# Key norm weights applied behind the transposition, and one finishing of the branch gates, in a hybrid attention layer

## The chip, the core and the metric

The kernel runs on one core of one Trainium2 chip. A core has five engines that run their own instruction streams and wait for each other by semaphores: TensorE (PE, matrix products and transpositions), VectorE (DVE), ScalarE (ACT), GpSimd (POOL) and SyncE (SP, which here issues transfers). The metric is the device time of one execution in microseconds (us). Some executions are also recorded by the hardware profiler; the span in a profile runs from the first to the last instruction.

## The reference

One decoder layer with 512 tokens, width 1024, heads of 64, all in float32. Two mixers read the same normalized input through one projection; their outputs are gated, projected and merged. Cut to what the change touches:

```python
def rms_norm(x, g):
    return x * lax.rsqrt(jnp.mean(x * x, axis=-1, keepdims=True) + EPS) * g

h = rms_norm(x, norm_w)
(q_a, k_a, v_a, z_a, q_b, kc, vc, ksl, vsl, kwn, vwn, gate_b, z_b, gate_m) = split(h @ w_in)
# mixer A: 8 heads, blocks of 256 keys
o_a = moba_mixer(rms_norm(heads(q_a), q_norm_a), rms_norm(heads(k_a), k_norm_a), heads(v_a), bias_a)
# mixer B: 8 query heads in 2 groups; compressed, selected and windowed keys
k_cmp = rms_norm(compress(heads(kc), ...), k_norm_cmp)
o_b = nsa_mixer(rms_norm(heads(q_b), q_norm_b), k_cmp, v_cmp,
                rms_norm(heads(ksl), k_norm_sel), heads(vsl),
                rms_norm(heads(kwn), k_norm_win), heads(vwn), gate_b, bias_b)
# inside nsa_mixer
g = jax.nn.sigmoid(branch_gate)      # 512 tokens x 8 heads x 3 branches
o = g[..., 0:1] * o_cmp + g[..., 1:2] * o_sel + g[..., 2:3] * o_win
```

The weights `g` of a norm are 64 numbers, one for each place within a head, the same for all tokens and heads. A score is the product of a query and a key, so a weight of the query's norm may as well be multiplied into the key's; the kernel does so.

## The kernel before

Tokens are handled in four tiles of 128. Every float32 product on PE is made of three faster ones: both operands are split into a rounded part and a rest (`wh` and `wl` for weights, `hh` and `hl` for the activations, `ks` and `kx` for keys, `ph` and `pl` for probabilities), and line 386 issues high by high, low by high and high by low. A weight tile arrives in `wr`, is rounded into `wh` by ACT (line 352), or by DVE or POOL (lines 354, 356), and its rest `wl` comes from DVE (line 361). The same goes for `vh` and `vl`, weights of the key compression.

The program is written as streams (projections, attention heads, compression of mixer B's keys) that a planner interleaves while the program is built: every step carries a cost for each engine on which it may run, and the planner puts each step on an engine and at a place in that engine's order by the times that these costs give. On the chip an engine works off its list in that order, so an instruction that waits holds all that is behind it on its engine.

The pieces around the change, by line:

- `load_consts` (line 1547) loads small tables: the tile `cst` (constants with one row for each partition, in two transfers of line 255) and `gn` (six vectors of norm weights, the same in all partitions). Four products on DVE (line 1560) then fold the query's weights and the score's factor 0.125 into the key's weights.
- `proj_norm` (line 737) projects one group of channels and norms it, token tile by token tile: `qk0` and `qk1` (each four query heads and four key heads of mixer A), then `kb` (four keys of mixer B, and its 24 gates a token), then `qb`. `norm` (line 709) is: scaled copy out of PSUM (`nraw`, line 718, ACT), square (720, ACT), sum by heads (721, DVE), factor and addition (426, DVE), inverse root (427, POOL), product with it (723, DVE or POOL), and then, for keys, the product with the weights `gn` (line 726 for mixer A, 729 for `kb`; DVE or POOL, whichever the planner found sooner).
- For `kb`, ACT takes the exponential of the negated gate into a small tile `ge` (line 745), and behind the norm DVE adds 1 (749) and takes the reciprocal (750) into the tile `gate`, 24 columns for each token tile: four such pairs in all.
- `k_pair` (line 969) brings two key heads into the form for scores: four transpositions on PE (`turn`, line 947) into a PSUM bank `pq`, of which 64 partitions belong to each head; two rounded copies for each head on ACT, into both halves of `ks` (line 978); the rest `kx` by a subtraction on DVE (line 980) out of the same bank; a copy of it into `kx`'s other half (line 983, ACT). It is called four times for mixer A and twice for mixer B: 24 copies and 12 subtractions. `k_pair`'s bank is of the kind that `q_pair`, the transpositions `pt` of probabilities and the sums `pu` of the compression (line 873) also use; it is free for the next once the last subtraction has read it.
- Scores: `sps` (lines 1024 and 1025) takes `ks` and `kx` against the split query; DVE adds the bias (`sb`, line 1043), ACT takes the exponential (`P`, line 1058), and PE transposes the probabilities (line 1071).
- Mixer B's small matrices are split too: `xs` (lines 706, 707) from the gathered input of the compression, `hs` (868), `gt` (878 to 882).

Of the kernel before, what the change touches and what calls it, by code (L numbers as in the profile page):

```python
# [19 lines left out]
D = 1024  # L20
# [10 lines left out]
COFF, NCST = {}, 0  # L31
for _n, _w in (("ident", P), ("ii", DH), ("cmask", NT * C32), ("rowv", NT), ("hmask", 2), ("pos", 32), ("w2", 256)):
    COFF[_n] = (NCST, _w)
    NCST += _w
# [72 lines left out]
def hybrid_kernel(ctx: ExitStack, tc: tile.TileContext, x, x0, xT, wtok, wchan, wz, wgate, gains, w1,  # L107
# [307 lines left out]

    ident = cview("ident")
    ii = cview("ii")
    cmask = cview("cmask").rearrange("p (b c) -> p b c", b=NT)
# [290 lines left out]
    def norm(ch, dst, ps, t, H, gi):  # L709
# [14 lines left out]
        if gi == 1:  # L724
            z = out[:, 4:]
            ch.do(either(256), lambda e: e.tensor_mul(z, z, gn[:, 1, :].unsqueeze(1).to_broadcast([P, 4, DH])))
        elif gi:
            z = out.rearrange("p (a b) d -> p a b d", a=2)
            ch.do(either(256), lambda e: e.tensor_mul(z, z, gn[:, gi:gi + 2, :].unsqueeze(2).to_broadcast([P, 2, 2, DH])))

# [6 lines left out]
    def proj_norm(name, gi, tags="gggg"):  # L737
        toks[name] = [None] * NT

        def emit(t, ps):  # L740
            toks[name][t] = att(name, F32)
            ch = Chain(now[0] + 230)
            if name == "kb":
                e_ = sp.tile([P, 24], F32, name=nm("ge"), tag="ge", bufs=4)
                ch.do({"A": 164}, lambda e: e.activation(e_, ps[:, 256:280], AF.Exp, scale=nrx[:, t:t + 1]))
            norm(ch, toks[name][t], ps, t, 4 if name == "kb" else 8, gi)
            if name == "kb":
                def g1(e):
                    e.tensor_scalar_add(e_, e_, 1.0)
                    e.reciprocal(gate[:, :, t], e_)  # L750
                ch.do({"D": 300}, g1)
            ch.mark(f"{name}.{t}")
        yield from gemm_tok(name, emit, tags)
# [214 lines left out]

    def k_pair(boxes, name, col, firsts=None):

# [5 lines left out]
        for r, (ks, kx) in enumerate(kk):  # L976
            for i in range(2):
                c.do({"A": 478}, lambda e, r=r, z=ks[64 * i:64 * i + 64, :]: e.copy(z, pt[64 * r:64 * r + 64, :]))
        for r, (ks, kx) in enumerate(kk):
            c.do({"D": 602}, lambda e, r=r, ks=ks, kx=kx: e.tensor_sub(  # L980
                kx[0:64, :], pt[64 * r:64 * r + 64, :], ks[0:64, :].bitcast(F32)), pt if r else None)
        for r, (ks, kx) in enumerate(kk):
# [176 lines left out]
    def moba_units():  # L1159
        us, qs, ks = [], [], [[], []]  # L1160
        for h in range(8):
            box = {}

            def pre(h=h, box=box):
                yield toks_of(f"qk{h // 4}")
                yield toks_of(f"v{h // 4}")
                if h % 2 == 0:
                    yield from q_pair(qs, f"qk{h // 4}", h % 4 * DH)
                    yield from k_pair(ks, f"qk{h // 4}", 256 + h % 4 * DH)
                yield need("rtab")  # L1170
# [10 lines left out]
    def nsa_units(g):  # L1181
# [3 lines left out]
        def pre0():  # L1185
            yield toks_of("kb")
            if not g:
                both.extend(att("kf").rearrange("p (i b c) -> p i b c", i=2, b=2) for _ in range(2))
                for br in range(2):
                    yield from k_pair(kbox, "kb", P * br, [z[:, :, br, :] for z in both])  # L1190
            yield toks_of("qb")
# [355 lines left out]
    def load_consts():  # L1547
# [11 lines left out]
        for i, k in ((0, 1), (2, 3), (2, 4), (2, 5)):  # L1559
            c.do({"D": 102}, lambda e, i=i, k=k: e.scalar_tensor_tensor(gn[:, k, :], gn[:, i, :], 0.125, gn[:, k, :], op0=ALU.mult,  # L1560
                                                                        op1=ALU.mult))

# [221 lines left out]
def _layout(inp):  # L1784
# [21 lines left out]
    onehot, cd = _consts()  # L1806
    cd.update(pos=posT.reshape(P, -1), w2=w2.reshape(P, -1))
    d = dict(x=f["x"][0], xT=f["x"][0].T[P:],
# [25 lines left out]
```

## Time and profile before

| what | value |
| --- | --- |
| time, median of 3 runs | 452.53 us (452.14 to 452.53) |
| profiled execution, its own time | 451.59 us |
| span in that profile | 449.8 us |
| granted TensorE clock, mean | 1.000 |
| PE busy / DVE / ACT / POOL | 441.8 / 384.0 / 302.9 / 198.9 us |
| products with k's weights (lines 726 and 729) | 9 on DVE, 3 on POOL |
| gate pairs (lines 749 and 750) | 4 on DVE |
| plain copies `ks` (line 978) | 24 on ACT |
| subtractions `kx` (line 980) | 12 on DVE |

Rows of the profile name an instruction as line, engine, operation, written tile `<-` read tiles, with partitions x elements. "Idle before" is the time that the engine stood still just before, with the row that released it. The profiled execution and the runs are separate executions, so a sum made from the profile's durations is held against 451.59, not against the median.

### The profile page before, as it was taken

How to read it: one execution, taken by the hardware profiler on the slowest of the kernel's cores; microseconds unless marked ns; L12 is line 12 of the kernel's file. 1: busy time of each engine (PE TensorE's matmuls, PEld its weight loads, DVE VectorE, ACT ScalarE, POOL GpSimd, SP SyncE). 2: the span in 40 equal slices, each digit the busy share in tenths (PEclk: the TensorE clock that was granted, in tenths of full speed). 3: DMA queues.
4: the chain of work that ended last, by engine and by line, in shares of the span. 5: the costliest groups of instructions: out<-in, count | busy, mean ns of one | idle time of the engine just before them, and what ended most of it. 6: DMA issues, size and time to landing. Idle time of an engine off the chain costs nothing.

```text
span 449.8 us, 8544 instructions
## 1 busy us (share of the span) xinstructions
PE 441.8 (98%) x2779; PEld 394.0 (88%) x2779; DVE 384.0 (85%) x943; ACT 302.9 (67%) x711; POOL 198.9 (44%) x235
## 2 busy tenths in 40 slices
PE   8999999999999999999999999999999999999997
PEld 7878888899778899888999998989988999998886
DVE  5999899899998797788899899977967699899783
ACT  6866778867978798376878677687764355454450
POOL 1153337865675573177675654764850222211000
PEclk9999999999999999999999999999999999999999
DMA  8975746887975879858978876986767878789872
GB/s 262 305 253 187 242 150 213 196 228 187 267 181 165 214 220 270 290 142 202 287 213 204 228 181 170 253 218 156 213 166 174 256 220 253 223 245 290 278 237 95
DMA packets 55086, 98.21 MB, mean 218 GB/s; under 512 B 5313, under 2 KB 9537, under 8 KB 55041
## 3 DMA queue, kind: packets, MB, share of 16 engines
q1 hardware_dynamic: 39808, 68.30, 47.2%
q0 software_dynamic: 7616, 14.68, 20.4%
q10 hardware_dynamic: 7616, 14.68, 9.7%
q8 instruction: 22, 0.36, 0.3%
q14 instruction: 24, 0.19, 0.1%
HBM read 90.69 MB, written 36.31 MB: 282 GB/s over the span
## 4 chain that ended last, share of the span: by engine, by line
PE 77%; DVE 12%; ACT 4%; issue 3%; DMA 2%; POOL 0%; SPq 0%; DVEq 0%; ACTq 0%
PE pgw L386 18%; PE pgt L386 14%; PE pbr L386 9%; PE po L386 9%; PE pgc L386 7%; PE O L1105 6%; PE pt L1071 5%; PE sps L1024 3%; PE sps L1025 3%; DVE wl L361 2%; DMA wr<-in_wgate 2%; DVE sb L1043 1%; DVE pl L1085 1%; DVE sq L490 1%; PE pq L947 1%
## 5 line engine op out<-in xcount | busy, mean ns | idle before, releaser
L361 DVE TENSOR_TENSOR wl<-wr,wh 128x512 fp32r<-128x512 f32 (+1 forms) x150 | 102.6, 701 | 2.1 <-ACT wh L352 1.8
L352 ACT CAST wh<-wr 128x512 fp32r<-128x512 f32 (+1 forms) x130 | 77.0, 608 | 15.3 <-DMA wr<-wsum 6.5
L356 POOL TENSOR_SCALAR wh<-wr 128x512 fp32r<-128x512 f32 (+1 forms) x39 | 31.6, 822 | 76.4 <-DVE wl L361 34.4
L1062 POOL TENSOR_SCALAR P<-P,sst,gate 128x512 f32<-128x512 f32 (+3 forms) x56 | 46.2, 828 | 40.0 <-DVE sst L1061 32.0
L1058 ACT ACTIVATE P<-sb,sst 128x512 f32<-128x512 f32 (+3 forms) x88 | 50.7, 577 | 17.5 <-DVE sst L1043 16.0
L1043 DVE CUSTOM_DVE_ANT_0 sb<-sps,T 128x512 f32<-128x512 f32 (+3 forms) x96 | 46.0, 483 | 14.0 <-PE sps L1025 13.5
L386 PE MATMUL pgt<-wh,hh 128*128 128x512 f32 (+2 forms) x160 | 56.6, 354 | 0.0
L386 PE MATMUL pgt<-wl,hh 128*128 128x512 f32 (+2 forms) x160 | 55.8, 349 | 0.8 <-DVE wl L361 0.8
L386 PE MATMUL pgt<-wh,hl 128*128 128x512 f32 (+2 forms) x160 | 55.7, 348 | 0.0
L386 PE MATMUL pgw<-th,wh 128*128 128x256 f32 x240 | 48.9, 281 | 0.3 <-DVE gm L1519 0.3
L1083 ACT CAST ph<-pt 128x512 fp32r<-128x512 f32 (+2 forms) x72 | 33.8, 476 | 19.8 <-PE pt L1071 18.5
L386 PE MATMUL pgw<-hh,wh 128*128 128x256 f32 x160 | 45.1, 282 | 0.5 <-ACT c L1460 0.5
L386 PE MATMUL pgw<-hl,wh 128*128 128x256 f32 x160 | 44.3, 277 | 0.0
L386 PE MATMUL pgw<-hh,wl 128*128 128x256 f32 x160 | 44.3, 277 | 0.0
L1071 PE MATMUL pt<-cst,P 128*128 128x128 f32 x232 | 40.7, 272 | 0.3 <-DVE pl L1085 0.3
L1085 DVE TENSOR_TENSOR pl<-pt,ph 128x512 fp32r<-128x512 f32 (+2 forms) x72 | 38.7, 549 | 1.8 <-ACT ph L1083 1.5
L386 PEld LDWEIGHTS pgw<-th,wh 128*128 128x128 f32 x240 | 39.4, 188 | 0.8 <-DVE gm L1519 0.5
L427 POOL TENSOR_TENSOR nr<-nss,mhalf 128x8 f32<-128x8 f32 (+1 forms) x16 | 26.4, 1650 | 22.5 <-DVE nss L426 19.3
L386 PEld LDWEIGHTS pgt<-wl,hh 128*128 128x128 f32 x160 | 30.0, 188 | 5.2 <-DVE wl L361 1.2
L386 PE MATMUL pgw<-th,wl 128*128 128x256 f32 x120 | 33.3, 277 | 0.0
L386 PEld LDWEIGHTS pgt<-wh,hh 128*128 128x128 f32 x160 | 30.1, 188 | 3.4 <-ACT nraw L718 0.2
L386 PEld LDWEIGHTS pgt<-wh,hl 128*128 128x128 f32 x160 | 30.1, 188 | 3.3
(271 smaller groups left out, 1289.4 us busy)
## 6 DMA issues: line engine op xcount, KB each, us to landing
wr<-wsum SPq DMA_DIRECT2D x56, 256.0 KB, 3.8
wr<-in_wtok SPq DMA_DIRECT2D x36, 256.0 KB, 4.8
wsum<-in_wgate ACTq DMA_DIRECT2D x16, 512.0 KB, 5.2
wsum<-wsum POOLq DMA_DIRECT2D x14, 512.0 KB, 7.6
wr<-in_wgate SPq DMA_DIRECT2D x24, 256.0 KB, 5.0
xsum<-th SPq DMA_DIRECT2D x16, 256.0 KB, 2.3
T<-rtab SPq DMA_DIRECT2D x16, 256.0 KB, 5.3
wr<-in_w SPq DMA_DIRECT2D x16, 256.0 KB, 4.3
```

The source lines that it names most:

```text
L352: e.copy(hi, raw)
L356: e.tensor_scalar(hi, raw, 1.0, 1.0, op0=ALU.mult, op1=ALU.mult)
L361: c.do({"D": cd(n)} if lead else either(n), lambda e, hi=hi, lo=lo, raw=raw: e.tensor_sub(lo, raw, hi.bitcast(F32))).mark((w, 1, i))
L386: nc.tensor.matmul(dst, sts[i][a], mvs[i][b], start=(start and i == a == b == 0), stop=(stop and i == n - 1 and b == 1), skip_group_check= ...
L427: c.do({"p": 430 + POWC * w}, lambda e: e.tensor_tensor(v(dst), v(ss), mhalf[:parts, :w], op=ALU.pow))
L1043: e.tensor_tensor_reduce(z["sb"][:, :L], sps[:, :L], T[:, S - L:], scale=-1.0, scalar=3e38, op0=ALU.add, op1=ALU.min, accum_out=st[:, 0, b ...
L1058: e.activation(pv(), z["sb"][:, :L], AF.Exp, bias=st[:, 0, b:b + 1], scale=-1.0, accum_out=st[:, 1, b:b + 1])
L1062: c.do({"P": 315 + 0.834 * L}, lambda e: e.tensor_scalar(pv(), pv(), st[:, 2, b:b + 1], g, op0=ALU.mult, op1=ALU.mult))
L1071: nc.tensor.transpose(pt[:, (b - kb) * P:(b - kb + 1) * P], u.p0 if u.p0 is not None and b == 0 else u.pb[:, POFF[b] + kb * P:POFF[b] + (k ...
L1083: e.copy(z["w"][0], pt[:, :w])
L1085: ch.do({"D": cd(w)}, lambda e: e.tensor_sub(z["w"][1], pt[:, :w], z["w"][0].bitcast(F32)), pt)
L1105: nc.tensor.matmul(O[0][:, S - n:], v.bitcast(F32) if kb == 3 else v, w, start=(u.first and kb == 0 and i == 0), stop=(u.last and kb == 3 ...
```

## The change

The keys of mixers A and B are no longer multiplied by their norm weights when they lie as tokens by channels. Behind the transposition a channel is a partition, so the weight is there one number for each partition: the constants get six columns more (`gcol`, the six weight vectors, each twice below the other for the two heads of a pair), the copy `ks` takes such a column as its scale, and the subtraction becomes (transposed key x column) - `ks` in one instruction. The steps of lines 726 and 729 stay in the planner with their costs and issue nothing; every other step keeps its engine and its place. Three of the four products in `load_consts` now work on columns of `cst`, and the first of them has to wait for the second transfer of `cst` and no longer for `gn`. The transfer of `gn` stays, and so does its product for the compressed keys, which are normed elsewhere (line 907).

Mixer B's gates: the exponential goes into `gate` itself, and the addition and the reciprocal run once, over all four token tiles (128x96), at the place of the fourth pair.

```diff
--- before.py
+++ after.py
@@ -29,7 +29,7 @@
 C32 = 32
 CMPH = 256
 COFF, NCST = {}, 0
-for _n, _w in (("ident", P), ("ii", DH), ("cmask", NT * C32), ("rowv", NT), ("hmask", 2), ("pos", 32), ("w2", 256)):
+for _n, _w in (("ident", P), ("ii", DH), ("cmask", NT * C32), ("rowv", NT), ("hmask", 2), ("gcol", 6), ("pos", 32), ("w2", 256)):
     COFF[_n] = (NCST, _w)
     NCST += _w
 POFF = [0, 128, 384, 768]
@@ -414,6 +414,7 @@
         return cst[:, o:o + n]
 
     ident = cview("ident")
+    gcol = cview("gcol")
     ii = cview("ii")
     cmask = cview("cmask").rearrange("p (b c) -> p b c", b=NT)
     rowv = cview("rowv")
@@ -722,11 +723,9 @@
         rsqrt_mean(ch, lambda: b["r"], lambda: b["ss"], DH, H)
         ch.do(either(n), lambda e: e.tensor_mul(out, b["raw"], b["r"].unsqueeze(2).to_broadcast([P, H, DH])), lambda: b["t"])
         if gi == 1:
-            z = out[:, 4:]
-            ch.do(either(256), lambda e: e.tensor_mul(z, z, gn[:, 1, :].unsqueeze(1).to_broadcast([P, 4, DH])))
+            ch.do(either(256), lambda e: None)
         elif gi:
-            z = out.rearrange("p (a b) d -> p a b d", a=2)
-            ch.do(either(256), lambda e: e.tensor_mul(z, z, gn[:, gi:gi + 2, :].unsqueeze(2).to_broadcast([P, 2, 2, DH])))
+            ch.do(either(256), lambda e: None)
 
     def hl4(t):
         return t.rearrange("p (h s d) -> p h s d", s=2, d=DH)
@@ -741,13 +740,13 @@
             toks[name][t] = att(name, F32)
             ch = Chain(now[0] + 230)
             if name == "kb":
-                e_ = sp.tile([P, 24], F32, name=nm("ge"), tag="ge", bufs=4)
-                ch.do({"A": 164}, lambda e: e.activation(e_, ps[:, 256:280], AF.Exp, scale=nrx[:, t:t + 1]))
+                ch.do({"A": 164}, lambda e: e.activation(gate[:, :, t], ps[:, 256:280], AF.Exp, scale=nrx[:, t:t + 1]))
             norm(ch, toks[name][t], ps, t, 4 if name == "kb" else 8, gi)
             if name == "kb":
                 def g1(e):
-                    e.tensor_scalar_add(e_, e_, 1.0)
-                    e.reciprocal(gate[:, :, t], e_)
+                    if t == NT - 1:
+                        e.tensor_scalar_add(gate, gate, 1.0)
+                        e.reciprocal(gate, gate)
                 ch.do({"D": 300}, g1)
             ch.mark(f"{name}.{t}")
         yield from gemm_tok(name, emit, tags)
@@ -966,7 +965,7 @@
                  pt if r else None)
             box.append((z, c))
 
-    def k_pair(boxes, name, col, firsts=None):
+    def k_pair(boxes, name, col, gi, firsts=None):
 
         yield room("t")
         pt = turn(name, col)
@@ -975,10 +974,12 @@
         kk = [(att("ks"), att("kx")) for _ in range(2)]
         for r, (ks, kx) in enumerate(kk):
             for i in range(2):
-                c.do({"A": 478}, lambda e, r=r, z=ks[64 * i:64 * i + 64, :]: e.copy(z, pt[64 * r:64 * r + 64, :]))
+                c.do({"A": 478}, lambda e, r=r, z=ks[64 * i:64 * i + 64, :]: e.activation(
+                    z, pt[64 * r:64 * r + 64, :], AF.Copy, scale=gcol[64 * r:64 * r + 64, gi:gi + 1]))
         for r, (ks, kx) in enumerate(kk):
-            c.do({"D": 602}, lambda e, r=r, ks=ks, kx=kx: e.tensor_sub(
-                kx[0:64, :], pt[64 * r:64 * r + 64, :], ks[0:64, :].bitcast(F32)), pt if r else None)
+            c.do({"D": 602}, lambda e, r=r, ks=ks, kx=kx: e.scalar_tensor_tensor(
+                kx[0:64, :], pt[64 * r:64 * r + 64, :], gcol[64 * r:64 * r + 64, gi:gi + 1], ks[0:64, :].bitcast(F32),
+                op0=ALU.mult, op1=ALU.subtract), pt if r else None)
         for r, (ks, kx) in enumerate(kk):
             c.do({"A": ca(512)}, lambda e, kx=kx: e.copy(kx[64:128, :], kx[0:64, :].bitcast(F32)))
             for i, z in enumerate((ks, kx) if firsts else ()):
@@ -1166,7 +1167,7 @@
                 yield toks_of(f"v{h // 4}")
                 if h % 2 == 0:
                     yield from q_pair(qs, f"qk{h // 4}", h % 4 * DH)
-                    yield from k_pair(ks, f"qk{h // 4}", 256 + h % 4 * DH)
+                    yield from k_pair(ks, f"qk{h // 4}", 256 + h % 4 * DH, 1)
                 yield need("rtab")
                 yield room("T")
                 box["T"] = load_bias(h)
@@ -1187,7 +1188,7 @@
             if not g:
                 both.extend(att("kf").rearrange("p (i b c) -> p i b c", i=2, b=2) for _ in range(2))
                 for br in range(2):
-                    yield from k_pair(kbox, "kb", P * br, [z[:, :, br, :] for z in both])
+                    yield from k_pair(kbox, "kb", P * br, 4 + br, [z[:, :, br, :] for z in both])
             yield toks_of("qb")
             for i in range(2):
                 yield from q_pair(box["q"], "qb", 256 * g + P * i)
@@ -1557,8 +1558,9 @@
         t = dma(cst[:, P:], consts[:, P:], 2000)
         c = Chain(t)
         for i, k in ((0, 1), (2, 3), (2, 4), (2, 5)):
-            c.do({"D": 102}, lambda e, i=i, k=k: e.scalar_tensor_tensor(gn[:, k, :], gn[:, i, :], 0.125, gn[:, k, :], op0=ALU.mult,
-                                                                        op1=ALU.mult))
+            z = gn.rearrange("p k d -> p d k") if k == 3 else gcol.unsqueeze(1)
+            c.do({"D": 102}, lambda e, i=i, k=k, z=z: e.scalar_tensor_tensor(z[:, :, k], z[:, :, i], 0.125, z[:, :, k], op0=ALU.mult,
+                                                                             op1=ALU.mult))
 
     def gemms():
         yield from proj_v("v", ("v0", "v1"), True)
@@ -1804,7 +1806,7 @@
                     for j in range(8)])
     wo = f["w_out"][0].reshape(2, 4, P, 2, 512).transpose(3, 0, 1, 2, 4).reshape(4, 4, P, 512)
     onehot, cd = _consts()
-    cd.update(pos=posT.reshape(P, -1), w2=w2.reshape(P, -1))
+    cd.update(gcol=np.tile(gains.reshape(6, DH).T, (2, 1)), pos=posT.reshape(P, -1), w2=w2.reshape(P, -1))
     d = dict(x=f["x"][0], xT=f["x"][0].T[P:],
              x0=np.concatenate([f["norm_w"][0].reshape(KT, P).T, f["x"][0].T[:P]], 1), wtok=wtok, wchan=wchan, wz=wz, wgate=wgate, gains=gains, w1=w1,
              relone=np.tile(np.concatenate([np.tile(f["rel_bias"], 8), onehot], 1), (2, 1)), wbr=wbr, wout=wo,
```

In the rows below, an engine's instructions stand in the order of its list; numbers behind a name only tell tiles apart. The first place is ACT while `kb` is normed, when the third pair of key heads of mixer A is brought in. Before:

```order
L745 ACTIVATE ge_1616<-pgt_1525,nrx 128x24
L706 CAST xs_1318<-XW_1317 128x4x64
L978 CAST ks_1608<-pq_1588 64x512
L718 ACTIVATE nraw_1641<-pgt_1525,rx 128x256
L352 CAST vh_1657<-wr_1556 128x512
L978 CAST ks_1610<-pq_1588 64x512
L720 ACTIVATE kb_1615<-nraw_1641 128x256
```

With the change:

```order
L743 ACTIVATE gate<-pgt_1515,nrx 128x24
L707 CAST xs_1310<-XW_1309 128x4x64
L977 ACTIVATE ks_1598<-pq_1578,cst 64x512
L719 ACTIVATE nraw_1629<-pgt_1515,rx 128x256
L352 CAST vh_1645<-wr_1546 128x512
L977 ACTIVATE ks_1600<-pq_1578,cst 64x512
L721 ACTIVATE kb_1605<-nraw_1629 128x256
```

All rows stay where they were; each copy `ks` reads `cst` as well, and the exponential writes `gate`.

The second place is DVE a little later: two splits `wl` of weights for the projection `qb`, with `gt` from the compression (its activation) and `sb`, the biased scores of a head. Before:

```order
L361 TENSOR_TENSOR wl_1725<-wr_1652,wh_1724 128x512
L729 TENSOR_TENSOR kb_1615<-kb_1615,gn 128x256
L882 SCALAR_TENSOR_TENSOR gt_1711<-gt_1711,pu_1707 128x128
L1043 ISA sb_1758,sst_1750<-sps_1745,T_1612 128x512
L1043 ISA sst_1750 128x1
L749 TENSOR_SCALAR ge_1616<-ge_1616 128x24
L750 RECIPROCAL gate<-ge_1616 128x24
L361 TENSOR_TENSOR wl_1713<-wr_1603,wh_1712 128x512
L1043 ISA sb_1775,sst_1750<-sps_1762,T_1612 128x384
```

With the change:

```order
L361 TENSOR_TENSOR wl_1707<-wr_1640,wh_1706 128x512
L881 SCALAR_TENSOR_TENSOR gt_1695<-gt_1695,pu_1691 128x128
L1044 ISA sb_1739,sst_1731<-sps_1726,T_1602 128x512
L1044 ISA sst_1731 128x1
L361 TENSOR_TENSOR wl_1697<-wr_1593,wh_1696 128x512
L1044 ISA sb_1754,sst_1731<-sps_1743,T_1602 128x384
```

The product with `gn` and the third gate pair, the one between `sb` and the next `wl`, are gone.

The third place is DVE behind that `wl`, where the fourth gate pair stood. Before:

```order
L1085 TENSOR_TENSOR pl_1784<-pt_1771,ph_1783 128x384
L1043 ISA sb_1793,sst_1750<-sps_1787,T_1612 128x256
L1043 ISA sst_1750 128x1
L1061 RECIPROCAL sst_1750<-sst_1750 128x1 x2
L749 TENSOR_SCALAR ge_1678<-ge_1678 128x24
L750 RECIPROCAL gate<-ge_1678 128x24
L1061 RECIPROCAL sst_1750<-sst_1750 128x1
```

With the change:

```order
L1086 TENSOR_TENSOR pl_1763<-pt_1750,ph_1762 128x384
L1044 ISA sb_1772,sst_1731<-sps_1766,T_1602 128x256
L1044 ISA sst_1731 128x1
L1062 RECIPROCAL sst_1731<-sst_1731 128x1 x2
L748 TENSOR_SCALAR gate<-gate 128x96
L749 RECIPROCAL gate<-gate 128x96
L1062 RECIPROCAL sst_1731<-sst_1731 128x1
```

The pair stands in the same place, over 96 elements instead of 24. On POOL three products with `gn` are gone; on PE and SP the order is the same.

## The prediction

> **What bounds the kernel now.** I read the busy times first, then a table by stage, then what TensorE (PE) waited for, then the chain of work that ended last inside the two stages where PE is not full.
>
> The page begins with the span and the busy times:
>
> ```profile
> span 449.8 us, 8544 instructions
> PE 441.8 (98%) x2779; PEld 394.0 (88%) x2779; DVE 384.0 (85%) x943; ACT 302.9 (67%) x711; POOL 198.9 (44%) x235
> ```
>
> PE is busy in 441.8 of 449.8 us, so all that any edit elsewhere can win is in some 8 us of gaps. VectorE (DVE), at 85%, counts only where a gap of PE waits for it. The table by stretches (start:end, length, then busy us of PE, of PE's weight loads, DVE, ScalarE (ACT), GpSimd (POOL), PE's clock, share of the DMA engines, GB/s) says where the gaps lie:
>
> ```profile
> 0.00:30.00 30.00, 28.42 (x143) 23.56 (x143) 24.28 (x45) 21.36 (x39) 7.76 (x18) 1.00 0.89 283
> 30.00:110.00 80.00, 79.91 (x433) 69.01 (x434) 73.51 (x178) 59.73 (x138) 45.47 (x51) 1.00 0.68 199
> 110.00:126.00 16.00, 14.00 (x84) 11.41 (x84) 15.84 (x43) 13.15 (x31) 8.73 (x8) 1.00 0.90 255
> 126.00:155.00 29.00, 29.00 (x160) 24.31 (x160) 24.70 (x74) 23.50 (x57) 18.74 (x21) 1.00 0.68 184
> 155.00:175.00 20.00, 19.77 (x163) 19.33 (x161) 14.88 (x37) 19.42 (x46) 10.99 (x13) 1.00 0.85 231
> 175.00:450.00 275.00, 270.65 (x1802) 246.42 (x1802) 230.81 (x570) 165.70 (x401) 107.23 (x127) 1.00 0.79 217
> ```
>
> All that the change edits runs before 175 us. From 30 to 110 and from 126 to 155 PE has no gap: there the other engines have slack. From 110 to 126 PE loses 2.0 us while DVE is busy in 15.84 of 16. From 155 to 175 PE loses only 0.23, but ACT is busy in 19.42 of 20, so nothing may be laid on it there. PE's waits name what each gap ended with (waiting line, releaser, us in all, times, longest):
>
> ```profile
> PE sps L1025 <- ACT kx L983: 1.0, 1, 1.0
> PE pgt L386 <- DVE wl L361: 0.8, 1, 0.8
> PE pu L873 <- DVE kx L980: 0.2, 1, 0.2
> ```
>
> The first two are in 110 to 126, the third ends the stretch 155 to 175. For that one the chain of waits, in order of time (start, us, what), reads:
>
> ```profile
> 155.15 0.69 ACT nraw L718
> ...
> 171.78 0.58 ACT ks L978
> ...
> 174.09 0.70 DVE kx L980
> ...
> 174.92 0.63 PE pu L873 x4
> ```
>
> It begins with a row that waited for PE and ends with PE waiting: a detour by ACT and DVE of 19.8 us, just longer than PE's own work beside it. Whatever is added to it moves PE.
>
> **The change part by part.** First the prices; the groups by line, of ACT (count, busy us, mean ns, then idle before):
>
> ```profile
> L978 ACT CAST ks<-pq 64x512 fp32r<-64x512 f32 x24 | 13.9, 580 | 0.4
> L718 ACT ACTIVATE nraw<-pgt,rx 128x512 f32<-128x512 f32 x12 | 8.2, 687 | 8.2 <-PE pgt L386 8.1
> L1083 ACT CAST ph<-pt 128x512 fp32r<-128x512 f32 x24 | 14.1, 585 | 17.3 <-PE pt L1071 17.1
> ```
>
> *The copies.* 24 plain copies `ks` become copies with a column as scale. The nearest row with such a column is `nraw`: same source (PSUM), same 512 elements, 687 ns against 585 for `ph`: +0.102 us, and I take that; the lower end is 0, in case a column costs less on 64 partitions. 24 x 0.102 = 2.4 us more on ACT, in six groups of four.
>
> The Trainium skill, "ScalarE: Activation LUTs", section "Step-by-step: what each stage is for", calls scale and bias a "Free affine" applied ahead of the lookup; taken as a statement of time it would make the ACT term nil (my first rival). The two rows above speak against it; the same page prices a pointer operand at about 93 ns in "What ACT_TABLE_LOAD costs", by which the eight copies that count below would come to 0.74 us where I reckon 0.82.
>
> The groups of DVE:
>
> ```profile
> L775 DVE SCALAR_TENSOR_TENSOR v<-pgf,rx,v 128x256 fp32r<-128x256 f32 x8 | 3.2, 470 | 0.0
> L1519 DVE TENSOR_TENSOR gm<-c,pgw 128x256 f32<-128x256 f32 x10 | 4.1, 414 | 0.0
> L980 DVE TENSOR_TENSOR kx<-pq,ks 64x512 fp32r<-64x512 f32 x12 | 8.2, 686 | 1.7 <-ACT ks L978 1.3
> L726 DVE TENSOR_TENSOR qk<-qk,gn 128x256 f32<-128x256 f32 x7 | 3.9, 550 | 0.0
> L729 DVE TENSOR_TENSOR kb<-kb,gn 128x256 f32<-128x256 f32 x2 | 0.8, 418 | 0.0
> L749 DVE TENSOR_SCALAR ge<-ge 128x24 f32<-128x24 f32 x4 | 1.0, 251 | 0.0
> L750 DVE RECIPROCAL gate<-ge 128x24 f32<-128x24 f32 x4 | 1.2, 306 | 0.1
> L1222 DVE RECIPROCAL cd<-cd 128x16 f32<-128x16 f32 x2 | 0.5, 244 | 0.0
> ```
>
> *The subtractions.* 12 `kx` get a column as second operand: 470 - 414 = 0.056 us each by the first two rows (lower end 0), 0.7 us in all.
>
> *The weights.* Nine products leave DVE (3.9 + 0.8 = 4.7 us); one of line 726 and two of line 729 leave POOL. *The gates.* Four pairs of 128x24 become one of 128x96. The reciprocal grows by (306 - 244)/8 = 7.8 ns an element, so to 0.306 + 72 x 0.0078 = 0.86 us; three pairs go (3 x 0.557 = 1.7), 0.55 comes back at the place of the fourth. DVE's relief is 4.7 + 1.7 - 0.55 - 0.7 = 5.1 us. Nearly all of it lies where PE is full, so it has to be followed stage by stage.
>
> *0 to 30 us.* Three of four gain products shrink from 64 elements to one, and the first now needs the constants. The transfers of that tile by line (first and last issue at the end), the transfer's own row (us to landing at the end) and the first product:
>
> ```profile
> L255 SPq DMA_DIRECT2D cst<-in_consts x2: 328/416/504, 9.6 to 11.6; - x2
> cst<-in_consts SPq DMA_DIRECT2D x1, 243.0 KB, 5.5
> 18.25 0.21 DVE L1560 SCALAR_TENSOR_TENSOR gn<-gn 128x64 f32<-128x64 f32 x1
> ```
>
> 11.6 + 5.5 = 17.1, some 1.1 us ahead of 18.25, and 3 KB more are 1% of the transfer. I cost this at nothing (at most 0.2 either way); past that margin the wait would hold the products behind it, which feed PE.
>
> *30 to 110 us.* Seven products of line 726 leave DVE (one more leaves POOL), and 8 of the copies each bring +0.10. PE has 0.09 us of gaps in 80, so the relief gains nothing; the copies may cost up to 0.1, I take 0.05. If PE's work were no cover here, the relief would be worth up to 3.9 us.
>
> *110 to 126 us.* Four copies, two products of line 729 on DVE, three gate pairs. The timeline of DVE, of POOL and of ACT (start, us, then as before):
>
> ```profile
> 114.80 0.41 DVE L729 TENSOR_TENSOR kb<-kb,gn 128x256 f32<-128x256 f32 x1
> 118.62 0.68 DVE L980 TENSOR_TENSOR kx<-pq,ks 64x512 fp32r<-64x512 f32 x1
> 123.91 0.53 DVE L749 TENSOR_SCALAR ge<-ge 128x24 f32<-128x24 f32 x1
> 124.69 1.07 DVE L361 TENSOR_TENSOR wl<-wr,wh 128x512 fp32r<-128x512 f32 x1
> 123.79 0.61 POOL L723 TENSOR_TENSOR kb<-nraw,nr 128x256 f32<-128x256 f32 x1
> 124.48 0.73 POOL L729 TENSOR_TENSOR kb<-kb,gn 128x256 f32<-128x256 f32 x1
> 114.19 0.41 ACT L706 CAST xs<-XW 128x256 fp32r<-128x256 f32 x1 [0.61 <-DVE XW L838]
> 117.85 0.58 ACT L978 CAST ks<-pq 64x512 fp32r<-64x512 f32 x1
> 121.14 1.14 ACT L983 CAST kx<-kx 64x512 fp32r<-64x512 f32 x2
> ```
>
> On ACT the first copy's +0.10 goes into the 0.61 idle before 114.19. From there to 121.14 ACT has no gap, and the other three copies make the `kx` copies 0.3 later: the wait of 1.0 grows to 1.3. On DVE the early removals (line 729 at 114.80, two gate pairs) do not add up, since the subtraction at 118.62 waits for the copy at 117.85, now 0.3 later, and the next split for an ACT copy: until 123 DVE stands about where it stood, perhaps 0.1 ahead. What does count is the third gate pair: it ran from 123.91 to 124.69, 0.78 us just ahead of the `wl` that PE waits for. Without it, `wl` starts near 123.85 and ends between 124.5 (at the group's usual 0.7) and 124.95 (if it meets POOL's line 723 as the old one met line 729). PE itself came 0.8 ahead of 125.81, at 125.01, and the 0.3 of the first wait does not reach this point, since a second gap stands between them, in which the weight loads of a transposition wait:
>
> ```profile
> 123.50 0.42 PEld L947 LDWEIGHTS pq<-cst,qk 128*128 128x128 f32 x4 [0.31 <-PE pt L1071]
> ```
>
> PE's own work there ended 0.31 before it started; what it waited for (the bank that DVE's rows at 123 free) comes no later than before, so this gap swallows the 0.3, and PE still arrives near 125.0. So PE goes on at 125.0 instead of 125.81: **-0.8**, between -0.3 (the 0.3 carried on, and a long `wl`) and -1.0.
>
> The stretched rows at 123.91 and 124.69 lie beside POOL's 123.79 and 124.48. The Trainium skill, "SBUF — State Buffer", section "SBUF: two separate sides", has a shared port pair as an exclusive lock for a whole instruction; by it `wl` would wait for line 723 to end at 124.40 and need 0.7 more, to 125.1, and the term would be -0.7.
>
> *126 to 155 us.* Four copies and the fourth gate pair, 0.55 longer. PE is full; ACT idles a microsecond after these copies:
>
> ```profile
> 142.99 0.21 ACT L916 CAST kcs<-pkt 128x64 fp32r<-128x64 f32 x1 [1.01 <-PE pkt L913]
> ```
>
> Cost nil; without that gap, 0.4. The gate pair stands behind `wl` and is followed by DVE's work for later heads; bounded at 0 to 0.2.
>
> *155 to 175 us.* Eight copies, all in the chain above, and its last subtraction: 8 x 0.102 + 0.056 = **+0.87** at PE's `pu`, which before waited only 0.2. Bounds: ACT's small gaps come to 20.00 - 19.42 = 0.58, of which 0.15 lies before 155.15; if the other 0.43 were slack, +0.44; if columns cost nothing, 0.
>
> After 175 nothing is edited; the shift is carried on. **Sum**: -0.8 + 0.05 + 0.87 = +0.1 us. The profiled execution took 451.59, so its like would take 451.7; the median of the runs is 452.53, 0.94 above it, and I add the change to that: **452.6**.
>
> **The rivals.** (a) *Faster*: the surcharge of the scale column doesn't reach PE, since it is absent or falls into ACT's gaps. Then 155 to 175 costs 0 to 0.4 and 110 to 126 gains 0.8 to 1.0: 452.53 - 1.0 = 451.5 to 452.1. For it: `pu` is late by 0.2 only. Against: `nraw`'s 687 ns, and ACT's 97% there.
>
> (b) *Slower*: 110 to 126 gives nothing, because the two waits there share one cause. ACT's copies, 0.3 later, hold PE at 121.8 and again the DVE rows behind, and `wl` starts no earlier and meets POOL; while 155 to 175 costs its 0.87. It decides from a `wl` that ends after 125.7: 452.53 + 0.05 + 0.87 = 453.45. For it: DVE's 15.84 of 16 us are work that waits for ACT at 118.62. Against: the 0.78 us stand directly before `wl`.
>
> (c) *Slower in another way*: the constants land later than 18.25 and DVE stands in the startup. Each microsecond past it is one on PE: 1 us late gives 453.6. The margin of 1.1 us speaks against it.
>
> (d) The change does not do what it says: the products stay as they were. The order of instructions shows them gone, so I give it nothing.
>
> **How the numbers follow.** About 0.2%, 0.9 us, is what a measurement of this kernel can tell from no change. Forecast (two terms that cancel, within 0.9): 0.72. Rival (a): 0.17, of which 0.02 stay within 0.9, so faster 0.15. Rival (b): 0.09, rival (c): 0.04, together slower 0.13. Within: 0.72. The range takes the net from -0.9 (a) to +1.0 (b): 451.6 to 453.5.
>
> **What would show it.** In the profile after, scaled `ks` at 0.68 us and `kx` at 0.74; DVE busy some 5 us less, ACT 2.4 more. PE's wait for `wl` near 125 gone or under 0.2, the wait for the copy `kx` near 122 at 1.2 to 1.4, the wait of `pu` near 175 at about 1.1 (not 0.2). Wrong would be: `ks` under 0.62 (rival a), a wait for `wl` that is still 0.5 or more (b), a row of DVE that waits for a transfer near 18 us (c), a new wait of PE in 30 to 110 or 126 to 155.

## The result, and the profile after

| | time before | time after | ratio after to before (95% interval) |
| --- | --- | --- | --- |
| median of 6 runs each | 452.31 us | 455.15 us (454.47 to 456.13) | 1.0064 (1.0047 to 1.0081) |

The changed kernel is slower by 0.64%, some 2.8 us. Forecast was no change, with a range that ended at 453.5. The profiled execution took 455.42 us, 3.83 more than the one of before. One of the six runs of a4, further down, took 1561.3 us and is left out of its ratio; nothing here shows why.

First the lines that answer to the prediction's steps. The profile's busy times and the table by stretches, of the changed kernel (columns as before):

```profile
span 453.6 us, 8528 instructions
PE 446.3 (98%) x2779; PEld 396.2 (87%) x2779; DVE 380.1 (84%) x928; ACT 305.6 (67%) x711; POOL 196.4 (43%) x232
...
0.00:30.00 30.00, 29.07 (x143) 23.61 (x143) 24.06 (x44) 21.56 (x39) 7.89 (x18) 1.00 0.88 280
30.00:110.00 80.00, 79.95 (x425) 68.09 (x425) 68.82 (x170) 60.46 (x138) 44.75 (x50) 1.00 0.66 198
110.00:126.00 16.00, 14.68 (x92) 12.20 (x91) 14.99 (x37) 13.13 (x30) 7.40 (x7) 1.00 0.88 240
126.00:155.00 29.00, 29.00 (x160) 24.19 (x159) 25.51 (x74) 24.36 (x59) 18.52 (x21) 1.00 0.74 199
155.00:175.00 20.00, 19.93 (x159) 19.07 (x158) 13.77 (x35) 18.78 (x42) 9.19 (x12) 1.00 0.74 199
175.00:450.00 275.00, 273.15 (x1806) 248.67 (x1806) 232.51 (x572) 167.35 (x405) 108.67 (x127) 1.00 0.80 219
```

ACT is busy 2.7 us more and DVE 3.9 less. PE's waits of the changed kernel:

```profile
PE sps L1026 <- ACT kx L984: 1.1, 1, 1.1
PE pu L872 <- DVE kx L980: 1.0, 1, 1.0
```

The wait of 0.8 for the split `wl` near 125 is gone, that of `pu` went from 0.2 to 1.0, that of `sps` from 1.0 to 1.1. The groups by line (ACT, DVE) and one row of DVE's timeline give the prices:

```profile
L977 ACT ACTIVATE ks<-pq,cst 64x512 fp32r<-64x512 f32 x24 | 16.4, 683 | 0.4
L980 DVE SCALAR_TENSOR_TENSOR kx<-pq,cst,ks 64x512 fp32r<-64x512 f32 x12 | 9.0, 748 | 3.2 <-ACT ks L977 3.0
...
128.09 0.75 DVE L749 RECIPROCAL gate<-gate 128x96 f32<-128x96 f32 x1
```

So the waits and the prices went the way that was forecast. And yet PE is busy 4.5 us longer. It is as full between 30 and 110 us as before (79.95 of 80), but it gets through the same work more slowly. The first row of that stretch and one at its end, of the kernel before:

```profile
30.39 0.40 PE L386 MATMUL pgt<-wh,hh 128*128 128x512 f32 x1
...
109.83 0.33 PE L1071 MATMUL pt<-cst,P 128*128 128x128 f32 x1
```

and the same two products with the change:

```profile
30.61 0.40 PE L386 MATMUL pgt<-wh,hh 128*128 128x512 f32 x1
...
111.22 0.33 PE L1072 MATMUL pt<-cst,P 128*128 128x128 f32 x1
```

79.44 us before, 80.61 after: 1.2 us lost in a stretch where PE never waits. It shows in the distance from one product's start to the next. Thirteen products in a row, of which four are shown, before:

```profile
44.03 0.39 PE L386 MATMUL pgt<-wh,hh 128*128 128x512 f32 x1
44.26 0.39 PE L386 MATMUL pgt<-wh,hl 128*128 128x512 f32 x1
44.49 0.39 PE L386 MATMUL pgt<-wl,hh 128*128 128x512 f32 x1
...
46.75 0.39 PE L386 MATMUL pgt<-wh,hh 128*128 128x512 f32 x1
```

and with the change:

```profile
43.91 0.40 PE L386 MATMUL pgt<-wh,hh 128*128 128x512 f32 x1
44.15 0.39 PE L386 MATMUL pgt<-wh,hl 128*128 128x512 f32 x1
44.38 0.40 PE L386 MATMUL pgt<-wl,hh 128*128 128x512 f32 x1
...
46.71 0.40 PE L386 MATMUL pgt<-wh,hh 128*128 128x512 f32 x1
```

Twelve distances take 2.72 us before and 2.80 after, 227 and 233 ns each, with records of the same length (0.39 and 0.40). When both traces are laid side by side product by product, the products that read `hh` or `hl` (some 1190) account for +4.1 us, the other 1520 for +0.35, and the gaps for -0.6: 3.8 us, the whole difference between the two executions. (Where a slow distance ends and a gap begins is a choice; it moves up to half a microsecond between the three shares.)

What sets these products apart is where their operands lie. `hh` and `hl` stand ahead of the constants in the on-chip memory, `wh`, `wl` and nearly all else behind them. The constants grew by 24 bytes a partition, which the allocation rounds to 32:

```text
byte in a partition     before    changed
hh                        2208       2208
hl                       18592      18592
cst                      35488      35488
first wh                 54944      54976
first wl                 57120      57152
```

(These are the starts of the tiles.) A product that reads `hh` has one operand that stayed and one that moved by 32 bytes. Products such as `po<-wh,mh` or `pbr<-yh,wh`, of which both operands moved, are as fast as before. So are the transpositions `pt<-cst,P`, though there too one operand stayed and the other moved: 109 ns from start to start over 128 columns in both kernels. Not every pair of operands is touched.

The places before were not just any. `SHIFT = 16` in the kernel (lines 37, 607, 619 and 622) sets some weight tiles 64 bytes into their buffers, and the rests `wl` of the others 128 bytes. In the built program the two operands of every product over 512 columns with `hh` or `hl` therefore lie a multiple of 256 bytes apart, those of `pgw` 64 or 192 bytes off such a multiple. The growth by 32 bytes broke this layout.

### The profile page after: what moved, and what is told of

Same layout as the page of the kernel before. It is cut to its first block, busy times and chain, and to the rows that moved or that the text cites. A ratio compares the mean times of both kernels' runs of the same rounds, so it can differ in the third digit from the quotient of the medians.

```text
span 453.6 us, 8528 instructions
## 1 busy us (share of the span) xinstructions
PE 446.3 (98%) x2779; PEld 396.2 (87%) x2779; DVE 380.1 (84%) x928; ACT 305.6 (67%) x711; POOL 196.4 (43%) x232
## 4 chain that ended last, share of the span: by engine, by line
PE 79%; DVE 9%; ACT 6%; issue 3%; DMA 2%; SPq 0%; ACTq 0%; DVEq 0%
PE pgw L386 19%; PE pgt L386 14%; PE pbr L386 10%; PE po L386 8%; PE pgc L386 7%; PE O L1106 6%; PE pt L1072 5%; PE sps L1026 3%; PE sps L1025 3%; DMA wr<-in_wtok 2%; ACT ks L977 1%; DVE wl L361 1%; PE pq L946 1%; DVE vl L361 1%; DMA xa<-in_x 1%
## 5 line engine op out<-in xcount | busy, mean ns | idle before, releaser
L361 DVE TENSOR_TENSOR wl<-wr,wh 128x512 fp32r<-128x512 f32 (+1 forms) x150 | 101.3, 693 | 4.6 <-ACT wh L352 4.2
```

The costliest lines, as they stand in the source:

```text
L361: c.do({"D": cd(n)} if lead else either(n), lambda e, hi=hi, lo=lo, raw=raw: e.tensor_sub(lo, raw, hi.bitcast(F32))).mark((w, 1, i))
```

## The experiments

The three sets below ran on different chips, each beside runs of the kernel before, and every ratio is to those.

Two theories. **Place**: the growth of the constants moved two operands against each other, and that alone is slow. **Edits**: the added work on ACT and DVE makes the loss in a way that the traces show badly.

**First set: place alone.** a1 adds an unused tile to the kernel before and changes no instruction; a2 adds the same to the changed kernel:

```diff
     cst = cp.tile([P, NCST], F32, name="cst")
+    cp.tile([P, 8], F32, name="pad")
     gn = cp.tile([P, 6, DH], F32, name="gn")
```

a3 puts it ahead of both `hh` and `hl` in the kernel before:

```diff
+    cp.tile([P, 8], F32, name="pad")
     hh = cp.tile([P, KT, S], F32R, name="hh")
     hl = cp.tile([P, KT, S], F32R, name="hl")
```

and a4 between the two:

```diff
     hh = cp.tile([P, KT, S], F32R, name="hh")
+    cp.tile([P, 8], F32, name="pad")
     hl = cp.tile([P, KT, S], F32R, name="hl")
```

a1:

> The kernel before, with an unused tile of 32 bytes a partition behind the constants; no instruction changes. Place theory (the change is slow because its constants grew and moved every tile behind them by 32 bytes against hh and hl): products that read hh or hl go from 227 to about 234 ns at 512 columns and from 113 to 118 at 256, the others stay, and the time rises by 3 to 4 us, to 455.5 to 456.5. Edit theory (the added work on ScalarE and VectorE is what costs): no change, 452.3 within 0.5.

a2:

> The changed kernel with the same unused tile behind its constants, so that what follows stands 64 bytes from its place before, instead of 32. Place theory: the products with hh and hl come back to 227 and 113 ns, and what is left is the edits alone, by the prediction's sum +0.1 us, so 451.5 to 453. Edit theory: as the changed kernel, 455.1. If 64 bytes are no better than 32, the products stay at 234 and the time at 455 too.

a3:

> The kernel before with the unused 32 bytes ahead of hh, so that all large tiles move together. If the place of the operands relative to each other counts, no change: 452.3, 227 ns. If each operand's own place counts (a start at an odd multiple of 32 bytes against a multiple of 64), all products change, by the sign seen in the changed kernel at least those with hh: other than 227 ns, and the time moves by 2 us or more. Edit theory: no change.

a4:

> The kernel before with the unused 32 bytes between hh and hl: hl moves with all that follows, hh stays. If the relative place of the two operands of one product counts, products with hh (two of three) go to 234 and 118 ns, those with hl stay at 227 and 113, and the time rises by two thirds of what the pad behind the constants costs, some 2 to 2.7 us. If it is the next stationary operand against the moving one that counts, products next to one with hh slow too and those with hl share it. Edit theory: no change.

Measured, with the two runs of the later sets that belong here (b1 and c1; their edits are below). A shift is that of everything behind the constants against `hh` and `hl`. The four columns in the middle are mean distances in ns from a product's start to the next of the same sum, where no wait lies between: `pgf` and `pgt` over 512 columns, which read `hh` or `hl` (some 350), `pgw` with `hh` or `hl` over 256 columns (some 450), and two kinds that read neither, `po` and `pbr` (276) and `pgw` with `th` (324). A row of a product names the operand that streams through PE first and the one that is loaded as its weights second: `pgf` and `pgt` stream the kernel's weights and load `hh` or `hl`, `pgw` does it the other way round.

```text
kernel   shift         hh/hl 512  hh/hl 256  others 512  others 256   time to before (95%)
before     0             228.1      114.3      228.6       114.7      1
a3         0 (all 32)    227.9      114.2      228.7       114.5      1.0008 (0.9992 to 1.0024)
a1        32             233.1      118.1      228.6       115.1      1.0055 (1.0038 to 1.0071)
changed   32             233.1      118.0      228.5       115.3      1.0064 (1.0047 to 1.0081)
a2        64             229.5      118.3      228.6       114.8      1.0044 (1.0027 to 1.0060)
b1       128             232.7      116.7      228.6       115.6      1.0047 (1.0030 to 1.0064)
c1       256             227.9      114.5      228.5       114.8      0.9998 (0.9984 to 1.0013)
a4        32 (hh only)   232.4      118.1      228.7       115.9      1.0051 (1.0033 to 1.0069)
```

a1 settles the main question: 32 unused bytes and not one instruction changed cost 0.55%, about as much as the whole change. Its busy times, and the same thirteen products as above, first and last:

```profile
PE 445.9 (98%) x2779; PEld 396.1 (87%) x2779; DVE 384.8 (85%) x943; ACT 302.7 (67%) x711; POOL 201.0 (44%) x235
...
44.05 0.39 PE L386 MATMUL pgt<-wh,hh 128*128 128x512 f32 x1
...
46.85 0.39 PE L386 MATMUL pgt<-wh,hh 128*128 128x512 f32 x1
```

Twelve distances take 2.80 us, as in the changed kernel. a3 moves the same tiles by the same 32 bytes together with `hh` and `hl`, and nothing happens: it is the distance between operands that counts, not the place of each. a1 cannot come from the edits, and the edit theory is out as the cause of the loss.

Two expectations failed. a2 did not come back: at 64 the wide products of the table are nearly as before, but the narrow ones are as slow as at 32. The width alone isn't what parts them: `pgc`, which is over 512 columns too but streams `hh` or `hl` and loads the weights, like `pgw`, goes from 229.7 ns before to 233.2 at 64. And in a4, where `hl` moved along with the weights and only `hh` stayed, the products with `hl` slowed too (`pgt<-wh,hl` alone: 228.2 to 231.5 ns, `pgw<-hl,wh`: 114.0 to 119.3). Products with `hh` and `hl` alternate, so the distance to the next start hangs on what a product's neighbours read as well; these runs don't tell which of the two it is that is held up.

**Second set: the parts of the change.** b1 to b3 were meant to stand at a harmless distance; 128 turned out not to be one. They still compare with each other.

b1 is the changed kernel with a wider unused tile:

```diff
     cst = cp.tile([P, NCST], F32, name="cst")
+    cp.tile([P, 24], F32, name="pad")
     gn = cp.tile([P, 6, DH], F32, name="gn")
```

b2 is b1 with the product of line 729 of before back in the norm, and in `k_pair` the scaled forms for mixer A only (the plain ones of before for mixer B):

```diff
         elif gi:
-            ch.do(either(256), lambda e: None)
+            z = out.rearrange("p (a b) d -> p a b d", a=2)
+            ch.do(either(256), lambda e: e.tensor_mul(z, z, gn[:, gi:gi + 2, :].unsqueeze(2).to_broadcast([P, 2, 2, DH])))
...
+                if gi == 1:
+                    c.do({"A": 478}, lambda e, r=r, z=ks[64 * i:64 * i + 64, :]: e.activation(
+                        z, pt[64 * r:64 * r + 64, :], AF.Copy, scale=gcol[64 * r:64 * r + 64, gi:gi + 1]))
+                else:
+                    c.do({"A": 478}, lambda e, r=r, z=ks[64 * i:64 * i + 64, :]: e.copy(z, pt[64 * r:64 * r + 64, :]))
...
-            z = gn.rearrange("p k d -> p d k") if k == 3 else gcol.unsqueeze(1)
+            z = gn.rearrange("p k d -> p d k") if k > 1 else gcol.unsqueeze(1)
```

b3 is b1 with the plain copy and the plain subtraction everywhere, so that it leaves the keys' weights out of the scores:

```diff
-                c.do({"A": 478}, lambda e, r=r, z=ks[64 * i:64 * i + 64, :]: e.activation(
-                    z, pt[64 * r:64 * r + 64, :], AF.Copy, scale=gcol[64 * r:64 * r + 64, gi:gi + 1]))
+                c.do({"A": 478}, lambda e, r=r, z=ks[64 * i:64 * i + 64, :]: e.copy(z, pt[64 * r:64 * r + 64, :]))
...
-            c.do({"D": 602}, lambda e, r=r, ks=ks, kx=kx: e.scalar_tensor_tensor(
-                kx[0:64, :], pt[64 * r:64 * r + 64, :], gcol[64 * r:64 * r + 64, gi:gi + 1], ks[0:64, :].bitcast(F32),
-                op0=ALU.mult, op1=ALU.subtract), pt if r else None)
+            c.do({"D": 602}, lambda e, r=r, ks=ks, kx=kx: e.tensor_sub(
+                kx[0:64, :], pt[64 * r:64 * r + 64, :], ks[0:64, :].bitcast(F32)), pt if r else None)
```

b4 is the kernel before with the gates' edit alone:

```diff
-                e_ = sp.tile([P, 24], F32, name=nm("ge"), tag="ge", bufs=4)
-                ch.do({"A": 164}, lambda e: e.activation(e_, ps[:, 256:280], AF.Exp, scale=nrx[:, t:t + 1]))
+                ch.do({"A": 164}, lambda e: e.activation(gate[:, :, t], ps[:, 256:280], AF.Exp, scale=nrx[:, t:t + 1]))
...
-                    e.tensor_scalar_add(e_, e_, 1.0)
-                    e.reciprocal(gate[:, :, t], e_)
+                    if t == NT - 1:
+                        e.tensor_scalar_add(gate, gate, 1.0)
+                        e.reciprocal(gate, gate)
```

b1:

> The changed kernel with 96 unused bytes behind its constants, so that all that follows stands 128 bytes from its place before. The runs so far put the cost on the distance between a product's two operands modulo 128 (512 columns: 227 to 229 ns at 0, 230.5 at 64, 233 at 32 and 96; 256 columns: 115 ns at 64, 118 elsewhere). By that, all products have the speeds of the kernel before, and the time is that of the edits alone: the -1.0 seen at the split wl near 125 and the +0.8 seen at pu near 175, so 452.0 to 452.6, the same as before within 0.2%. If a distance of 128 is no better than 64: 454.6 again.

b2:

> As b1, but the weights of mixer B's windowed and selected keys stay in the norm (line 729 of before), and the two k_pairs of mixer B copy plainly; mixer A and the gates as changed. If the eight scaled copies between 155 and 175 us are what lengthens ScalarE's stretch there, the wait of pu comes back from 1.0 to 0.2 and the time is 0.8 to 0.9 below b1, near 451.4; the products of line 729 stand under TensorE's work and cost 0 to 0.4 in 110 to 126. If that wait is no cost (hidden later), as b1.

b3:

> As b1, but all copies ks and subtractions kx are plain; the weights of the keys of mixer A and of the windowed and selected keys are left out of the scores. Copies at 580 ns and subtractions at 686, no surcharge anywhere: the wait of sps falls from 1.1 to 0.9 or less, that of pu to 0.2, and the time is 0.9 to 1.2 below b1, near 451.2. If the surcharge is no cost, as b1.

b4:

> The kernel before with only the gates' edit (one pair over 128x96). By the prediction's term the third pair, 0.78 us just ahead of the split wl that TensorE waits for near 125, is what counts: the wait of 0.8 goes or falls below 0.3, and the time is 0.5 to 0.8 below before, 451.5 to 451.8. If the products of line 729 are needed for that too, the wait stays above 0.4 and the gain is under 0.4.

**Third set: the same three at 256 bytes** (the unused tile is 56 numbers instead of 24, nothing else differs from b1, b2 and b3).

c1:

> The changed kernel with 224 unused bytes behind its constants, so that all that follows stands 256 bytes from its place before. With b1 the distance of 128 turned out not to be like 0 (232 against 228 ns at 512 columns), so the pattern is longer than 128. If it repeats at 256, the products with hh and hl come back to 227 to 229 and 114 to 115 ns, and the time is that of the edits alone: b4's gain by the gates, 1.4, less the 0.8 that pu waits longer and some 0.3 at sps, so 451.8 to 452.6. If not, products stay slow and the time is near 454.7 as in b1.

c2:

> As b2 (weights of the windowed and selected keys left in the norm, plain copies in mixer B), with the distance of 256 bytes. b2 was 1.05 below b1 at equal distance. If the distance repeats at 256: 1 below c1, so 450.9 to 451.5. If it doesn't: near 453.6 as b2.

c3:

> As b3 (all copies and subtractions plain, weights of the keys left out of the scores), with the distance of 256 bytes. b3 was 1.6 below b1. If the distance repeats at 256: near b4, 450.7 to 451.3, since what the two differ in (products of lines 726 and 729) stood under TensorE's work. If it doesn't: near 453.1 as b3.

Measured:

```text
kernel                                   median   ratio to before (95%)
b1  the change, shift 128                454.69   1.0047 (1.0030 to 1.0064)
b2  as b1, mixer B's weights in the norm 453.64   1.0030 (1.0017 to 1.0042)
b3  as b1, plain copies                  453.08   1.0013 (1.0000 to 1.0027)
b4  before, gates finished once          450.88   0.9964 (0.9949 to 0.9979)
c1  the change, shift 256                452.45   0.9998 (0.9984 to 1.0013)
c2  as c1, mixer B's weights in the norm 451.70   0.9975 (0.9961 to 0.9990)
c3  as c1, plain copies                  450.54   0.9954 (0.9936 to 0.9972)
```

c1 is the changed kernel with another 224 bytes left empty. It is 2.7 us faster than without them, by the medians, and within its interval as fast as the kernel before: **the edits themselves come to nothing that these runs can tell, the loss is the place.** At c1 the products with `hh` and `hl` are back at 227.9 and 114.5 ns. The two edits that matter show in PE's waits and rows where the prediction had put them. c1's waits:

```profile
PE sps L1027 <- ACT kx L985: 1.1, 1, 1.1
PE pu L873 <- DVE kx L981: 1.0, 1, 1.0
```

and two rows of PE's timeline, of the kernel before:

```profile
125.81 0.49 PE L386 MATMUL pgt<-wl,hh 128*128 128x512 f32 x1 [0.80 <-DVE wl L361]
...
174.92 0.63 PE L873 MATMUL pu<-cst,hs 128*128 128x64 f32 x4 [0.23 <-DVE kx L980]
```

and of c1:

```profile
125.33 0.40 PE L386 MATMUL pgt<-wl,hh 128*128 128x512 f32 x1
...
175.79 0.63 PE L873 MATMUL pu<-cst,hs 128*128 128x64 f32 x4 [1.02 <-DVE kx L981]
```

The first has no wait in brackets any more, the second one of 1.02. Product by product, c1's PE was 0.52 us later than before's at 110 us and 0.58 earlier at 126, so it gained 1.1 there; at 175 it was 0.87 later, so it lost 1.45 between. Behind that its profile falls back by another 0.9 by the end, which nothing here explains; that execution took 453.38, 0.9 above c1's median.

c2 takes the scaled copies out of mixer B alone, and the wait of `pu` is back at the old size. c2's waits:

```profile
PE sps L1032 <- ACT kx L990: 1.1, 1, 1.1
...
PE pgw L386 <- DVE gm L1526: 0.8, 2, 0.6
...
PE pu L874 <- DVE kx L987: 0.2, 1, 0.2
```

It is 0.75 us faster than c1 by the medians (b2: 1.05 faster than b1). The 1.45 and the 0.75 differ in part because c2 has the products of line 729 back: in its profile 110 to 126 gains 0.72, not 1.1. c3, without any scaled copy, is 1.9 faster than c1 (b3: 1.6 than b1), and equal to b4 within the intervals. So the scaled columns cost 1.6 to 1.9 us, and the gates' edit wins about as much (b4: 1.4 by the medians). That c3, which has no products with `gn` in the norm, is no faster than b4, which has all twelve, says that taking them out won nothing that can be told. b4, which leaves the keys' weights where they were and so lets the constants be, is the fastest kernel that computes the reference, 0.36% below before (0.21% to 0.51%). Some of what it wins early is given back: where the kernel before had no wait at 289 us, b4 has one of 0.45 for a row of DVE in the merge of the mixers. (The profiled execution of b4 took 451.79, 0.9 above its median, so this may weigh less in the others.)

```profile
PE pgw L386 <- DVE gm L1519: 0.7, 2, 0.5
```

Of the expected sizes, several were missed though the direction held: b4 won 1.4 where 0.5 to 0.8 stood, b3 was 1.6 below b1 and not 0.9 to 1.2, and c2 and c3 ended 0.2 outside what was expected of them.

## Why the prediction was wrong, point by point

- **The step that failed** stands under "0 to 30 us": the growth of the constants was costed as a transfer ("3 KB more are 1% of the transfer. I cost this at nothing"). The transfer was indeed harmless; no row of DVE waits for it near 18 us. But the constants are also a place in memory, and what follows them moved by 32 bytes. That cost 2.5 us (a1) of the 2.8 measured, and no term of the sum and no rival held it. `SHIFT`, in the printed kernel, says that places had been set; the prediction doesn't speak of it.
- **A second error let the first one through**: "PE is full" was read as "PE is at its best". In 30 to 110 and in the long stretch after 175, where "nothing is edited; the shift is carried on", PE had no gaps that an edit could fill, but its products could get slower. There lie most of the 4.1 us that the products with `hh` and `hl` lost.
- **-0.8 at `wl`**: right in kind, a little small. The wait is gone in the changed kernel, in c1 and in b4; c1 gained 1.1 in that stage. The gap of 0.31 ahead of the transposition, which the prediction had swallow the first wait's growth, went too. The growth itself was 0.1, not 0.3.
- **+0.87 at `pu`**: right in kind, and too small. PE's wait there is 1.0 as forecast (about 1.1), but c1 lost 1.45 in the stage, since besides the 0.8 more at `pu` some 0.6 came ahead of it, at 163 to 167 us, which the prediction did not have. c2's profile has none of the 1.45, so the scaled copies and subtractions of mixer B are its cause; which row passes on the earlier part was not settled.
- **The prices** were close: copies +0.103 us (683 against 580; forecast 0.102), subtractions +0.062 (748 against 686; 0.056), the reciprocal over 96 elements 0.75 (0.86). DVE's busy time fell by 3.9 us and not by the 5.1 reckoned; where the difference went was not followed. The "Free affine" of the Trainium skill, "ScalarE: Activation LUTs", section "Step-by-step: what each stage is for", says nothing of time; what the same page of the Trainium skill has for a pointer operand in "What ACT_TABLE_LOAD costs", about 93 ns, is near the 103 measured.
- **`wl` against POOL**: in the changed kernel `wl` took its usual 0.69 and the product of line 724 on POOL was stretched instead, to 1.01 from 0.61:

```profile
125.24 0.69 DVE L361 TENSOR_TENSOR wl<-wr,wh 128x512 fp32r<-128x512 f32 x1
...
125.39 1.01 POOL L724 TENSOR_TENSOR kb<-nraw,nr 128x256 f32<-128x256 f32 x1
```

  The one that started first kept its speed, as the Trainium skill, "SBUF — State Buffer", section "SBUF: two separate sides", has it of the shared port pair; here DVE was first by 0.15 us. In b4 POOL was first by 0.11, at 124.05: its product kept 0.61, and `wl` took 1.04. In the rows above POOL's product ended 0.47 us after `wl`, less than its own 0.61, so they don't show that it stood still all that time.
- **The sum of the edits**, +0.1 us, is what c1 measured: -0.1, with an interval of -0.7 to +0.6. That is luck in part: in c1's profile the two terms were too small by 0.3 and 0.6, and by the medians by more (the gates 1.4 against 0.8, the scaled columns 1.6 to 1.9 against 0.92), and the errors nearly cancel.
- **The rivals**: none was right. The result left the range on the slow side, where (b) and (c) had stood with some 453.5, but neither happened: no stage lost its gain, and no transfer was late.

## What to carry to other kernels

An edit that adds a tile or widens one moves all that is allocated behind it; compare the addresses of the two programs before reading anything else into a difference, look in the kernel for constants that set places, and hold a padded version (here 224 unused bytes) against the edited one. Where an engine is busy without gaps, compare the distances between the starts of equal instructions in both traces: busy shares cannot show that each has become 2 to 3% longer. And a change of several edits is worth taking apart even when its sum is nothing: here one of them alone won 0.36%.

## What the runs showed of the hardware

For the products with `hh` or `hl`, the distance from one start to the next on PE depended on how far apart the places of the two operands lie in a partition. Against the kernel before, in which it was 228 ns for `pgf` and `pgt` over 512 columns, a further shift by 32 bytes gave 233, by 64 gave 229.5, by 128 gave 232.7, by 256 gave 227.9; for `pgw` over 256 columns 114.3, then 118, 118.3, 116.7 and 114.5. These are not one pattern seen at two widths: before, the operands of the first kind lie a multiple of 256 bytes apart, those of `pgw` 64 or 192 off it, and the two kinds have streamed and loaded operand exchanged. `pgc`, with 512 columns and the operands exchanged as in `pgw`, had 229.7, then 232.8, 233.2, 232.2 and 229.8. And `pgt` over 256 columns, which also starts 64 or 192 off, hardly moved: 118.0, then 118.2, 117.6, 117.5 and 118.0. So neither the distance nor the width alone says what a product costs; the role of the operands differs too, and how the three act together was not taken apart.

All had come back at 256 bytes; whether the period is exactly that was not tried, nor other distances, nor what inside the chip makes it. It is a property of the place and not of an execution: kernels at equal distances have these means within 0.5 ns on different edits (before, a3, b4 and c1), and the granted clock was 0.999 or 1.000 in all the profiled executions. In a profile the effect has no wait, no releaser and no gap; the durations of the records hide most of it too.
